# Order of TensorE's small products in an RWKV-7 recurrence: heads in turns, outputs by shape, a narrow projection on all rows

## The chip, the cores and the metric

The kernel runs on one core of one Trainium2 chip. The metric is the device time of one execution in microseconds (us); the median of three runs is given.

## The reference

A two-layer decoder trunk over 1024 tokens of 1024 channels in float32. Layer 0 is forgetting attention with a pooling mixer, layer 1 is RWKV-7 time mixing; each is followed by a SwiGLU feed-forward part with 2816 hidden channels. The change touches layer 1 alone:

```python
w = -jax.nn.softplus(-(w0 + jnp.tanh(xw @ w1) @ w2)) - 0.5      # narrow projections: 1024 -> 64 -> 1024
a = jax.nn.sigmoid(a0 + (xa @ a1) @ a2)
...
def _rwkv7_step(state, inp):                                     # 16 heads of 64 channels, 1024 tokens
    r_t, w_t, k_t, v_t, a_t, b_t = inp
    sa = jnp.einsum('bhvk,bhk->bhv', state, a_t)
    state = state * w_t[:, :, None, :] + sa[..., None] * b_t[:, :, None, :] + v_t[..., None] * k_t[:, :, None, :]
    return state, jnp.einsum('bhvk,bhk->bhv', state, r_t)
```

## The kernel before

Values lie with the channels on the partitions and the tokens along the free axis, in two halves of 512 tokens. A large product is made of 128x128 blocks of weights that are split into a high and a low part (`load_part`, lines 150 and 151: a copy on ScalarE, a difference on VectorE) and three passes on TensorE (`mm3`, lines 162 to 164). One such pass over 512 tokens is called a **fill pass** below.

The recurrence is cut into chunks of 64 tokens. `job(grp, half)` does four pairs of heads over half of the tokens; there are four jobs. A pair has one head on partitions 0 to 63 and the other on 64 to 127. A job has three stages:

- **Preparation**, pair by pair. After some elementwise work come the scores (line 1056: for each head two tiles of four products, 64 rows by 128 columns of the array, each 128 wide), their evictions (lines 1060 on ScalarE, 1061 and 1063 on VectorE), the transposes of `bk` (line 1069: eight for each head, 64 rows by 128 columns, 64 wide) and the values less their mean (line 1079: 64 rows by 64 columns, the two heads in turns). The tiles of the scores come from a pool of three PSUM banks (tag `s`), those of the transposes and values from a pool of two (tag `o`).
- **Inverses** of triangles, mostly 30 steps on VectorE (lines 1104 and 1106).
- **Chunks**, eight in a row: `z` (line 1159) and its copy, `u` (line 1165) and its copies, `sp` (line 1171), the next state on VectorE (lines 1173 to 1178), and the output `yp` (lines 1182 and 1184). Lines 1159, 1171 and 1182 use 128 rows by 64 columns, lines 1165 and 1184 use 64 by 64. In `yp` the two shapes take turns: two products of line 1182, two of line 1184, four times over.

Each job is woven with feed-forward work or projections: wherever the job says `yield n`, n more fill passes are emitted (`weave`; the numbers are in `fr`). The framework's scheduler then places each engine's instructions by readiness and priority, so the order on TensorE is its order, not quite the written one. A float32 product of the recurrence is one instruction in the program and two in the trace; a transpose is one in both.

The dense part of the layer (`dense`) has two narrow projections (`lora`), each with a hidden width of 64, for each half of the tokens. Their hidden values are stacked: high parts on rows 0 to 63 and low parts on rows 64 to 127 of a tile `t`, and the weights lie twice above each other. Each of eight blocks is a product of 128 rows (line 854) and one of 64 rows (line 855).

Of the kernel before, what the change touches and what calls it, by code (L numbers as in the profile page):

```python
# [19 lines left out]
S = 1024  # L20
# [7 lines left out]
# columns of the per-channel vector array  # L28
# [12 lines left out]
# columns of the constant array  # L41
# [34 lines left out]
def xtile(k, pool):  # L76
    """A tile of a half of the tokens with one column before them."""
    return pool.tile([P, HN + 1], F32, tag="x", name=nm(k, "x"), bufs=8)
# [46 lines left out]
def pmm(k):  # L125
    """A bank for a dense product of the stream that is being emitted."""
    pool, tag, bufs = k.mm
    return pool.tile([P, HN], F32, tag=tag, name=nm(k, tag), bufs=bufs)
# [6 lines left out]
def load_w(k, ap, tag="w", w=512, bufs=None, pool=None):  # L135
    """Loads a block of weights, 512 columns at a time, and splits each into two parts of which the sum is the block."""
    p, n = ap.shape
    return [load_part(k, ap[:, c:c + min(512, n)], p, min(512, n), tag, w, bufs, pool) for c in range(0, n, 512)]
# [16 lines left out]
def mm3(k, out, pairs, first=True, last=True):  # L155
    """out = sum of (wh + wl)^T (xh + xl) without wl^T xl, which is below float32's last bit.

    A generator: it yields the passes that it has put on the tensor engine."""
    nc = k.nc
    n = len(pairs)  # L160
    for i, ((wh, wl), (xh, xl)) in enumerate(pairs):
        nc.tensor.matmul(out, wh, xh, start=(first and i == 0), stop=False)  # L162
        nc.tensor.matmul(out, wh, xl, start=False, stop=False)  # L163
        nc.tensor.matmul(out, wl, xh, start=False, stop=(last and i == n - 1))  # L164
        yield 3


def narrow(k, out, n, w, xs):
    """float32 products with n columns of weights: 128 / n groups of columns of the array sum over a part of the inputs each."""
    g = P // n  # L170
    for c in range(0, len(xs), g):
        for q in range(g):
            j = c + q
# [5 lines left out]
def fold(k, out, src, n, tmp):  # L179
    """The sum of what narrow left in the groups of rows of src, on the first n rows."""  # L180
# [8 lines left out]
def run(gen):  # L189
    """Emits all of a generator; returns what it returns."""  # L190
# [12 lines left out]
def stream(k, i):  # L203
    """What follows runs where the streams of a lower number leave room."""
# [5 lines left out]
def ahead(fill, n):  # L210
    """Emits the first n passes of fill."""
    while n > 0:
        n -= next(fill)


def weave(main, *fills):
    """Emits main with as many passes of the fills as it asks for; a fill comes with its share, or alone."""
# [9 lines left out]
def using(k, gen, **own):  # L227
    """gen with settings of its own."""
# [20 lines left out]
def pair(k, pool, tag, bufs, n=HN):  # L249
    """The tiles of the two parts of a value."""  # L250
# [12 lines left out]
def use_ln_exp(k, after=None):  # L263
    """Has Exp and Ln read one table; after: the instruction whose table it replaces."""
# [6 lines left out]
def head_mean(k, sq, hl, more):  # L271
    """Mean over the channels of each head of a pair and a product more; hl: tiles for the parts of sq."""
# [8 lines left out]
class Norm:  # L281
    """RMS norm over the channels of [channel, token] tiles of one half of the tokens."""
# [30 lines left out]
def fox(k, ins, H, hpool, xpools, y, then, r_att):  # L313
    """The mixer of the first layer; y gets the tiles of its output, H those of its input.

    The projections take the tokens before their RMS norm; what it divides them by comes in behind the products.
    then runs beside the last pair of heads."""
# [22 lines left out]
    # of every half of the tokens: one over their root mean square, and what the heads' norms add for their own eps  # L340
# [34 lines left out]
    # operand tiles of the two heads of a pair  # L375
# [22 lines left out]
    def forget(half, wf):  # L398
        """Log sigmoid of the forget gates, running sums over the tokens."""
# [15 lines left out]
    def key_bias():  # L415
        """The running sums with the tokens on the partitions, negative."""
# [7 lines left out]
    def head(p, which, half, hl):  # L424
        """The queries or keys of a pair of heads."""
# [18 lines left out]
    def gate(p, half, hl):  # L444
        """The output's gate waits in the tile of the output."""
# [10 lines left out]
    def prep(p):  # L456
        """Projections of a pair of heads."""
# [37 lines left out]
    def maxima(p, a):  # L495
        h = 2 * p + a
        # cum of the keys along the free axis
# [26 lines left out]
    def attend(p, a):  # L524
        """Keys on the partitions, queries along the free axis; the values' products run behind the scores'."""
# [53 lines left out]
    def pool_group(g, half):  # L579
# [9 lines left out]
        # the mean over the tokens of a window comes after the product with the group's weights  # L589
# [92 lines left out]
def ffn(k, ins, L, halves, H, X, acc, tp, groups, after=None, silu=True, fb0=0):  # L682
# [25 lines left out]
    # the products with the third weights of a group run behind the first ones of the next  # L708
# [32 lines left out]
class Rwkv:  # L741
    """Time mixing of the second layer.

    The state runs over chunks of 64 tokens.  With L the running sum of the log decays inside a chunk,
    alpha_t = kk_t exp(L_{t-1}), beta_s = -kk_s a_s exp(-L_s), kt_s = k_s exp(-L_s), rt_t = r_t exp(L_t):
        U = (I - tril(alpha beta^T, -1))^-1 (alpha S + tril(alpha kt^T, -1) V)
        Y = rt S + tril(rt beta^T) U + tril(rt kt^T) V
        S <- exp(L_end) (S + beta^T U + kt^T V)
    The group norm's mean is taken off V, of whose rows every row of Y is a sum.
    """  # L750
# [11 lines left out]
    # ---- dense part  # L762
    def norm(self, half, rs, xt):
        """Puts the normalised tokens in the place of x, those of the token before beside them."""
# [35 lines left out]
    def sigmoid(self, t, src, j=None):  # L800
        """The sigmoid of src and column j of the vectors."""
# [8 lines left out]
    def dense(self, half, hd, mp, tp, which=((2, "k", 1), (3, "v", 4), (0, "r", 5))):  # L810
        """All projections of half of the tokens; the small ones run between the large ones."""
# [10 lines left out]
        def stacked(mx, w, n, func):  # L822
            """The hidden values of a narrow projection, high parts above low parts (above high parts)."""
# [23 lines left out]
        def lora(mx, w1, w2, func, c0, n):  # L847
            t = yield from stacked(mx, ins[w1], 64, func)
            for m in range(KT):
# [5 lines left out]
                nc.tensor.matmul(o, lo[0:64, c], t[0:64], start=False, stop=True)  # L855
# [3 lines left out]
        def stacked_w(w):  # L859
            """Weights for stacked hidden values: high parts twice above low parts."""  # L860
# [7 lines left out]
        def gate(mx, ts):  # L868
# [3 lines left out]
            for m in range(KT):  # L872
                # the first blocks start with what is there before the second part of the hidden values
# [28 lines left out]
        # a small projection runs among the blocks of a large one  # L902
# [22 lines left out]
    # ---- core  # L925
# [35 lines left out]
    def await_(self, n):  # L961
        """Asks for passes of the fills until n is there."""
# [3 lines left out]
    def head_sum(self, src):  # L966
        """The mean over the channels of each head of a pair."""
# [16 lines left out]
    def job(self, grp, half):  # L984
        """Four pairs of heads over half of the tokens.

        The rows of head h of a pair: its own half of the partitions (64 h to 64 h + 64) has what is summed over
        its channels or multiplies U, the other half what multiplies V, so that one product sums over both."""
# [14 lines left out]
        for i, p in enumerate(pr):  # L1003
# [6 lines left out]
            if i == 0:  # L1010
                ZL = [big(f"ZL{h}", 128) for h in range(2)]    # own: alpha | rt, other: alpha kt^T | rt kt^T
                XR = big("XR", 128)                            # own: inverse | rt beta^T
                SV = [big(f"SV{h}", 64) for h in range(2)]     # own: state, other: V
                BK = [big(f"BK{h}", 64) for h in range(2)]     # own: beta, other: kt
# [13 lines left out]
            # 1 / max(norm, 1e-12); what the bias adds is nothing beside 1e-24  # L1028
# [22 lines left out]
            # scores with the keys on the partitions: beta above kt, alpha beside rt  # L1051
            for h in range(2):
                for b in range(2):
                    sc = pst(k, "s", k.sbufs)
                    for c in range(4):
                        nc.tensor.matmul(sc[:, 128 * c:128 * c + 128], bk[HS[h], 4 * b + c], ZL[h][HS[h], i, 4 * b + c],  # L1056
                                         start=True, stop=True)
                    s4 = sc.rearrange("p (c t) -> p c t", t=128)
                    bs = slice(4 * b, 4 * b + 4)
# [6 lines left out]
            for h in range(2):  # L1066
                pt = pst(k, "o", 2)
                for c in range(8):
                    nc.tensor.transpose(pt[:, 64 * c:64 * c + 64], bk[HS[h], c], ident[HS[h], HS[h]])
# [15 lines left out]
        # inverses of the unit triangles: 32 x 32 blocks by substitution, one block a partition  # L1085
# [9 lines left out]
        # what lies above the diagonal, in squares, and the diagonal  # L1095
# [53 lines left out]
        for c in range(8):  # L1149
# [30 lines left out]
            for i in range(4):  # L1180
                for h in range(2):
                    nc.tensor.matmul(yp[HS[h], i], SV[h][:, i, c], ZL[h][:, i, c, 64:128], start=True, stop=False)  # L1182
                for h in range(2):
                    nc.tensor.matmul(yp[HS[h], i], uv[h][HS[h], i], XR[HS[h], i, c, 64:128], start=False, stop=True)  # L1184
# [5 lines left out]
        # the variances of all heads on a few rows, one over their roots in two parts there, then back to all rows  # L1190
# [39 lines left out]
def build(ctx, tc, ins, outs, dbg=None, stop=99):  # L1230
# [30 lines left out]
    # first layer's mixer  # L1261
# [23 lines left out]
    def oproj_early():  # L1285
        """What the output projection can do before the last pair of heads is there."""
# [91 lines left out]
    def tail(half, p, ng, silu):  # L1378
        """The last output projection and what follows it, for half of the tokens."""
# [76 lines left out]
def layout(inputs):  # L1456
    """The inputs in the order that the loads want."""
# [87 lines left out]
```

## Time and profile before

| | before |
|---|---|
| median of three runs | 2766.65 us (2763.74 to 2767.2) |
| span of the profiled execution, first to last instruction | 2762.1 us |
| PE (TensorE) busy | 2712.5 us (98%) |
| DVE (VectorE) busy | 1728.4 us (63%) |
| ACT (ScalarE) busy | 1300.0 us (47%) |
| mean granted TensorE clock | 0.998 |

The profiled execution has no time of its own beside its span; the span is 4.5 us below the median of the runs, which is what lies around it. Busy time of TensorE counts overlapping matmuls once. In the timeline the first column is the start of an instruction or of a run of like ones, the second its length to the end of the last; since matmuls overlap, what a matmul takes from the next is read from start to start.

### The profile page before, as it was taken

The page shows a single profiled execution, that of the slowest core. Times are in us where ns is not written, and L with a number is a line of the kernel's source. Part 1 is how long each engine was busy: PE and PEld are TensorE (multiplying, and loading weights), DVE is VectorE, ACT ScalarE, POOL GpSimd, SP SyncE. Part 2 cuts the span into 40 slices and gives each one's busy share as a digit, 9 for nine tenths or more (in the row PEclk, how much of TensorE's full clock was granted, in tenths as well). Part 3 has the DMA queues.
Part 4 walks back from the last instruction along what each step waited for, and adds up shares of the span by engine and source line. Part 5 has one row for each costly group of instructions (what it writes and reads, how often), then busy time and mean ns, then how long its engine had stood idle before and what let it go on. Part 6 is the DMA issues. An engine that isn't in the chain of part 4 may idle for free.

```text
span 2762.1 us, 40277 instructions
## 1 busy us (share of the span) xinstructions
PE 2712.5 (98%) x15368; PEld 2099.0 (76%) x15368; DVE 1728.4 (63%) x2940; ACT 1300.0 (47%) x2297; POOL 50.9 (2%) x139
## 2 busy tenths in 40 slices
PE   9999999999999999999999999999999999999999
PEld 6777778778887667777777676777777777788887
DVE  7777685653436655975984675469668846544343
ACT  7555664442225665434534466664445434333222
POOL 1000000000001000000000000000000000000000
PEclk9999999999999999999999999999999999999999
DMA  4111131233333445424433525454244235333332
GB/s 133 60 47 61 40 96 46 88 94 93 95 96 110 164 154 182 129 83 124 142 92 93 189 94 159 156 181 124 82 127 142 81 96 191 107 97 99 96 99 92
DMA packets 170241, 306.11 MB, mean 111 GB/s; under 512 B 18608, under 2 KB 25904, under 8 KB 170048
## 3 DMA queue, kind: packets, MB, share of 16 engines
q1 hardware_dynamic: 156224, 278.38, 32.8%
q10 hardware_dynamic: 13824, 25.17, 2.5%
q8 instruction: 120, 1.97, 0.3%
q14 instruction: 73, 0.60, 0.1%
HBM read 257.04 MB, written 46.43 MB: 110 GB/s over the span
## 4 chain that ended last, share of the span: by engine, by line
PE 84%; DVE 9%; ACT 2%; issue 2%; DMA 2%; SPq 0%; ACTq 0%; DVEq 0%
PE mm L162 17%; PE mm L163 16%; PE mm L164 16%; PE fm L162 7%; PE fm L164 6%; PE fm L163 6%; DVE wlo L151 2%; PE s L1056 2%; PE o L1184 1%; PE mm L174 1%; PE o L1182 1%; DVE nu L1106 1%; DVE pd L1104 1%; PE o L1171 1%; PE s L1159 1%
## 5 line engine op out<-in xcount | busy, mean ns | idle before, releaser
L150 ACT CAST whi<-wraw 128x512 fp32r<-128x512 f32 x738 | 453.4, 616 | 875.0 <-PE mm L163 494.5
L151 DVE TENSOR_TENSOR wlo<-wraw,whi 128x512 fp32r<-128x512 f32 x738 | 501.2, 683 | 465.7 <-ACT whi L150 454.2
L162 PE MATMUL mm<-hh,whi 128*128 128x512 f32 x864 | 344.8, 401 | 6.7 <-ACT hh L354 6.2
L164 PE MATMUL mm<-hh,wlo 128*128 128x512 f32 x864 | 340.3, 394 | 0.0
L163 PE MATMUL mm<-hl,whi 128*128 128x512 f32 x864 | 339.2, 394 | 0.0
L162 PE MATMUL mm<-uh,whi 128*128 128x512 f32 x728 | 289.2, 399 | 0.9 <-DVE x L1312 0.9
L164 PE MATMUL mm<-uh,wlo 128*128 128x512 f32 x728 | 287.1, 395 | 0.9 <-DVE wlo L151 0.9
L163 PE MATMUL mm<-ul,whi 128*128 128x512 f32 x728 | 287.3, 396 | 0.0
L162 PE MATMUL fm<-h1h,whi 128*128 128x512 f32 x528 | 217.6, 412 | 10.1 <-DVE sg L725 6.0
L164 PE MATMUL fm<-h1h,wlo 128*128 128x512 f32 x528 | 207.7, 393 | 0.0
L163 PE MATMUL fm<-h1l,whi 128*128 128x512 f32 x528 | 207.6, 393 | 0.1
L162 PEld LDWEIGHTS mm<-hh,whi 128*128 128x128 f32 x864 | 162.8, 189 | 43.2 <-ACT hh L354 6.9
L164 PEld LDWEIGHTS mm<-hh,wlo 128*128 128x128 f32 x864 | 162.7, 188 | 36.0 <-DVE wlo L151 0.4
L163 PEld LDWEIGHTS mm<-hl,whi 128*128 128x128 f32 x864 | 163.1, 189 | 33.1 <-DVE hl L355 1.1
L162 PE MATMUL fm<-hh,whi 128*128 128x512 f32 x416 | 173.6, 417 | 1.9 <-ACT hh L258 1.9
L162 PEld LDWEIGHTS mm<-uh,whi 128*128 128x128 f32 x728 | 136.3, 187 | 42.2 <-issue 7.0
L163 PE MATMUL fm<-hl,whi 128*128 128x512 f32 x416 | 166.3, 400 | 0.2 <-DVE hl L259 0.2
L164 PE MATMUL fm<-hh,wlo 128*128 128x512 f32 x416 | 166.0, 399 | 0.0
L163 PEld LDWEIGHTS mm<-ul,whi 128*128 128x128 f32 x728 | 136.5, 187 | 34.9 <-issue 1.1
L164 PEld LDWEIGHTS mm<-uh,wlo 128*128 128x128 f32 x728 | 136.5, 187 | 34.3 <-DVE wlo L151 1.3
L704 DVE TENSOR_TENSOR x<-mm,x 128x512 f32<-128x512 f32 x96 | 66.2, 692 | 122.9 <-PE mm L164 122.6
L162 PEld LDWEIGHTS fm<-h1h,whi 128*128 128x128 f32 x528 | 98.9, 187 | 42.6 <-issue 8.8
(338 smaller groups left out, 4731.0 us busy)
## 6 DMA issues: line engine op xcount, KB each, us to landing
wraw<-in_wg_dram SPq DMA_DIRECT2D x176, 256.0 KB, 2.8
wraw<-in_wu_dram SPq DMA_DIRECT2D x176, 256.0 KB, 2.7
wraw<-in_wd_dram SPq DMA_DIRECT2D x176, 256.0 KB, 2.7
wraw<-in_w_in_dram SPq DMA_DIRECT2D x52, 256.0 KB, 3.0
x<-in_xT_dram SPq DMA_DIRECT2D x32, 256.0 KB, 4.8
x<-x SPq DMA_DIRECT2D x32, 256.0 KB, 3.8
wraw<-in_w_k_dram SPq DMA_DIRECT2D x32, 256.0 KB, 2.9
wraw<-in_w_v_dram SPq DMA_DIRECT2D x32, 256.0 KB, 2.8
```

The costliest lines, as they stand in the source:

```text
L150: k.nc.scalar.copy(hi[0:p, 0:n], raw[0:p, 0:n])
L151: k.nc.vector.tensor_tensor(lo[0:p, 0:n], raw[0:p, 0:n], rd(hi[0:p, 0:n]), ALU.subtract)
L162: nc.tensor.matmul(out, wh, xh, start=(first and i == 0), stop=False)
L163: nc.tensor.matmul(out, wh, xl, start=False, stop=False)
L164: nc.tensor.matmul(out, wl, xh, start=False, stop=(last and i == n - 1))
L174: k.nc.tensor.matmul(out[n * q:n * q + n], w[:, n * j:n * j + n], xs[j], start=c == 0, stop=c + g == len(xs), tile_position=(0, n * q))
L704: nc.vector.tensor_tensor(X[half][m], o, X[half][m], ALU.add)
L1056: nc.tensor.matmul(sc[:, 128 * c:128 * c + 128], bk[HS[h], 4 * b + c], ZL[h][HS[h], i, 4 * b + c], start=True, stop=True)
L1104: nc.vector.tensor_tensor(pv, nu[:, j + 1:32, j:j + 1].broadcast_to([P, n, j]), nu[:, j:j + 1, 0:j].broadcast_to([P, n, j]), ALU.mult)
L1106: nc.vector.tensor_tensor(nu[:, j + 1:32, 0:j], nu[:, j + 1:32, 0:j], pv, ALU.add)
L1159: nc.tensor.matmul(z[HS[h], i], ZL[h][:, i, c, 0:64], SV[h][:, i, c], start=True, stop=True)
L1171: nc.tensor.matmul(sp[HS[h], i], BK[h][:, i, c], uv[h][:, i], start=True, stop=True)
```

## The change

The two heads of a pair take turns in the scores and in the transposes, so that the banks of a pair's scores are asked for two at a time, and both banks of its transposes at once. The products of `yp` come in two groups, eight of line 1182 and then eight of line 1184; the first of each head's column group starts the sums and the last ends them. The low weights of a narrow projection are multiplied by all 128 rows of `t`, which adds their product with the low parts. Comments are left out throughout the new file; of that nothing is shown.

```diff
@@ lora
                 nc.tensor.matmul(o, hi[:, c], t, start=True, stop=False)
-                nc.tensor.matmul(o, lo[0:64, c], t[0:64], start=False, stop=True)
+                nc.tensor.matmul(o, lo[:, c], t, start=False, stop=True)
@@ job
-            for h in range(2):
-                for b in range(2):
-                    sc = pst(k, "s", k.sbufs)
-                    for c in range(4):
-                        nc.tensor.matmul(sc[:, 128 * c:128 * c + 128], bk[HS[h], 4 * b + c], ZL[h][HS[h], i, 4 * b + c],
+            for b in range(2):
+                scs = [pst(k, "s", k.sbufs) for _ in range(2)]
+                for c in range(4):
+                    for h in range(2):
+                        nc.tensor.matmul(scs[h][:, 128 * c:128 * c + 128], bk[HS[h], 4 * b + c], ZL[h][HS[h], i, 4 * b + c],
                                          start=True, stop=True)
-                    s4 = sc.rearrange("p (c t) -> p c t", t=128)
-                    bs = slice(4 * b, 4 * b + 4)
+                bs = slice(4 * b, 4 * b + 4)
+                for h in range(2):
+                    s4 = scs[h].rearrange("p (c t) -> p c t", t=128)
...
-            for h in range(2):
-                pt = pst(k, "o", 2)
-                for c in range(8):
-                    nc.tensor.transpose(pt[:, 64 * c:64 * c + 64], bk[HS[h], c], ident[HS[h], HS[h]])
+            pts = [pst(k, "o", 2) for _ in range(2)]
+            for c in range(8):
+                for h in range(2):
+                    nc.tensor.transpose(pts[h][:, 64 * c:64 * c + 64], bk[HS[h], c], ident[HS[h], HS[h]])
+            for h, pt in enumerate(pts):
...
             yp = i3(pst(k, "o", 2))
-            for i in range(4):
-                for h in range(2):
-                    nc.tensor.matmul(yp[HS[h], i], SV[h][:, i, c], ZL[h][:, i, c, 64:128], start=True, stop=False)
-                for h in range(2):
-                    nc.tensor.matmul(yp[HS[h], i], uv[h][HS[h], i], XR[HS[h], i, c, 64:128], start=False, stop=True)
+            for i, h in ihs:
+                nc.tensor.matmul(yp[HS[h], i], SV[h][:, i, c], ZL[h][:, i, c, 64:128], start=i == 0, stop=False, skip_group_check=True)
+            for i, h in ihs:
+                nc.tensor.matmul(yp[HS[h], i], uv[h][HS[h], i], XR[HS[h], i, c, 64:128], start=False, stop=i == 3, skip_group_check=True)
```

The scheduled order on TensorE for a pair's scores (`s<-ZL,bk`), transposes (`o<-cc,bk`) and values (`o<-cc,ld`), third pair of the last job, before; rows of fill passes are left out where "..." stands:

```order
L1056 MATMUL s_19606<-ZL_4170_19109,bk_19594 128x128 x4
L1056 MATMUL s_19631<-ZL_4170_19109,bk_19594 128x128 x4
L1056 MATMUL s_19645<-ZL_4171_19110,bk_19594 128x128 x4
...
L1056 MATMUL s_19667<-ZL_4171_19110,bk_19594 128x128 x4
...
L1069 MATMUL o_19684<-cc,bk_19594 128x64 x8
...
L1069 MATMUL o_19708<-cc,bk_19594 128x64 x8
...
L1079 MATMUL o_19725<-cc,ld_19602 64x64 x16
```

The same pair with the change:

```order
L1057 MATMUL s_19606<-ZL_4170_19109,bk_19594 128x128
L1057 MATMUL s_19607<-ZL_4171_19110,bk_19594 128x128
...
L1057 MATMUL s_19606<-ZL_4170_19109,bk_19594 128x128
L1057 MATMUL s_19607<-ZL_4171_19110,bk_19594 128x128
L1057 MATMUL s_19645<-ZL_4170_19109,bk_19594 128x128 x4
...
L1057 MATMUL s_19646<-ZL_4171_19110,bk_19594 128x128 x4
L1071 MATMUL o_19684<-cc,bk_19594 128x64
L1071 MATMUL o_19685<-cc,bk_19594 128x64
...
L1082 MATMUL o_19725<-cc,ld_19602 64x64 x16
```

The first eight products take turns. The next two tiles do not: with three banks only one of them can be had, so one head's four products follow in a row, and the other head's four come after the first bank has been emptied. The sixteen transposes stand together. Over all 16 pairs, the stretches in which scores, transposes or values interrupt the fill passes go from 75 to 61, and the number of fill passes in each stage stays the same.

The output of the first chunk of the first job on TensorE, before, behind the products of `sp` (line 1171):

```order
L1182 MATMUL o_10960<-ZL_2218_9416,SV_2221_9419 64x64
L1182 MATMUL o_10960<-ZL_2219_9417,SV_2222_9420 64x64
L1184 MATMUL o_10960<-XR_9418,uv_10897 64x64
L1184 MATMUL o_10960<-XR_9418,uv_10898 64x64
L1182 MATMUL o_10960<-ZL_2218_9416,SV_2221_9419 64x64
L1182 MATMUL o_10960<-ZL_2219_9417,SV_2222_9420 64x64
```

The end of it with the change:

```order
L1185 MATMUL o_10960<-ZL_2219_9417,SV_2222_9420 64x64
L1185 MATMUL o_10960<-ZL_2218_9416,SV_2221_9419 64x64
L1185 MATMUL o_10960<-ZL_2219_9417,SV_2222_9420 64x64
L1187 MATMUL o_10960<-XR_9418,uv_10897 64x64
L1187 MATMUL o_10960<-XR_9418,uv_10898 64x64
L1187 MATMUL o_10960<-XR_9418,uv_10897 64x64
L1187 MATMUL o_10960<-XR_9418,uv_10898 64x64
```

All products of one shape stand together; what comes ahead of them and behind them in a chunk has not moved.

## Rows read from the trace of the kernel before

**Rows 1.** The page, part 1: busy time, share, instructions of each engine.
```profile
PE 2712.5 (98%) x15368; PEld 2099.0 (76%) x15368; DVE 1728.4 (63%) x2940; ACT 1300.0 (47%) x2297; POOL 50.9 (2%) x139
```

**Rows 2.** Windows: stretch, length; PE, PEld, DVE, ACT, POOL busy; clock; DMA share; GB/s.
```profile
910.00:950.00 40.00, 40.00 (x160) 29.09 (x159) 21.95 (x34) 27.71 (x49) 0.00 (x0) 1.00 0.57 188
1074.00:1142.00 68.00, 64.79 (x446) 49.20 (x444) 63.88 (x101) 38.70 (x72) 4.53 (x9) 1.00 0.49 154
...
1213.00:1290.00 77.00, 77.00 (x823) 56.72 (x822) 35.96 (x70) 29.59 (x64) 0.79 (x2) 1.00 0.32 94
1307.00:1372.00 65.00, 63.10 (x420) 48.52 (x419) 61.25 (x96) 38.31 (x69) 1.99 (x7) 1.00 0.51 158
...
1815.00:1890.00 75.00, 71.70 (x448) 55.22 (x447) 62.94 (x100) 49.11 (x88) 3.18 (x9) 0.98 0.56 180
...
2066.00:2140.00 74.00, 74.00 (x485) 56.04 (x485) 66.38 (x103) 41.23 (x77) 2.89 (x7) 1.00 0.48 145
```

**Rows 3.** Timeline, PE, first chunk: start, length, instruction, shape, count.
```profile
1213.67 0.69 PE L1159 MATMUL s<-SV,ZL 128*64 128x64 f32 x16
1214.29 0.50 PE L162 MATMUL fm<-h1h,whi 128*128 128x512 f32 x1
...
1215.88 0.68 PE L1165 MATMUL s<-zs,XR 64*64 64x64 f32 x16
1216.49 0.50 PE L162 MATMUL fm<-h1h,whi 128*128 128x512 f32 x1
...
1218.75 0.69 PE L1171 MATMUL o<-uv,BK 128*64 128x64 f32 x16
1219.27 0.29 PE L1182 MATMUL o<-ZL,SV 128*64 128x64 f32 x4
1219.48 0.33 PE L1184 MATMUL o<-XR,uv 64*64 64x64 f32 x4
...
1221.33 0.50 PE L971 MATMUL t<-ph,bones 128*128 128x512 f32 x1
...
1223.38 0.69 PE L1159 MATMUL s<-SV,ZL 128*64 128x64 f32 x16
```

**Rows 4.** Timeline, DVE, the next chunk's state.
```profile
1220.42 0.86 DVE L1177 TENSOR_TENSOR SV<-st,Pc 64x256 f32<-64x256 f32 x2
```

**Rows 5.** Timeline, PE, third pair of the last job.
```profile
2109.32 2.60 PE L1056 MATMUL s<-ZL,bk 64*128 64x128 f32 x24
2111.86 0.49 PE L164 MATMUL fm<-gh,wlo 128*128 128x512 f32 x1
2112.28 1.16 PE L1056 MATMUL s<-ZL,bk 64*128 64x128 f32 x8
2113.37 0.50 PE L162 MATMUL fm<-gh,whi 128*128 128x512 f32 x1
...
2114.27 0.71 PE L1069 MATMUL o<-cc,bk 64*128 64x64 f32 x8
2114.91 0.50 PE L162 MATMUL fm<-gh,whi 128*128 128x512 f32 x1
```

**Rows 6.** Timeline, PE, two score tiles in a row, third job.
```profile
1846.94 2.05 PE L1056 MATMUL s<-ZL,bk 64*128 64x128 f32 x16
1848.92 0.51 PE L163 MATMUL fm<-hl,whi 128*128 128x512 f32 x1
```

**Rows 7.** Timeline, PE, the longest wait of a score tile for its bank.
```profile
1089.22 1.13 PE L1056 MATMUL s<-ZL,bk 64*128 64x128 f32 x8 [1.31 <-DVE ZL L1063]
```

**Rows 8.** Timeline, PE, one block of a narrow projection between fill passes.
```profile
912.55 0.39 PE L854 MATMUL mm<-st,wlhi 128*128 128x512 f32 x1
912.89 0.50 PE L855 MATMUL mm<-st,wllo 64*128 64x512 f32 x1
913.32 0.50 PE L162 MATMUL mm<-uh,whi 128*128 128x512 f32 x1
913.65 0.39 PE L163 MATMUL mm<-ul,whi 128*128 128x512 f32 x1
913.88 0.40 PE L164 MATMUL mm<-uh,wlo 128*128 128x512 f32 x1
```

**Rows 9.** Groups by line and shape, PE: count, busy us, mean ns, idle before.
```profile
L855 PE MATMUL mm<-st,wllo 64*128 64x512 f32 x32 | 15.9, 498 | 0.0
```

## The prediction

> **What bounds the kernel now.** I read the page's busy times first: TensorE is busy for 98% of the span [rows 1], so what it no longer does is time gained, unless it then waits. Whether it would wait differs by stage, so I read the windows next [rows 2]. In a chunk stage (1213 to 1290, one of four) TensorE is busy all 77.00 us and VectorE 35.96: TensorE alone sets the pace. The same holds among the blocks of a narrow projection (910 to 950). In the preparation of pairs it is otherwise: VectorE has 63.88 of 68 us, 61.25 of 65, 62.94 of 75 and 66.38 of 74. There both engines are nearly full, and a gain on TensorE is worth at most what VectorE has left. Last I read the timelines, start to start, because busy times hide how far matmuls overlap. They show one thing that carries most of the sum: TensorE pays whenever the shape of its tiles changes. A fill pass starts 0.23 us after the one before it [rows 8]; around other shapes the steps are longer.
>
> **The outputs, by shape.** Before, 16 products of `yp` run from 1219.27 to 1221.33, which is 2.06 us, with eight changes of shape counting the one that leaves [rows 3]. For the new order each group has a neighbour of its own shape and number. Line 1185 continues the shape of `sp`: 16 instructions of line 1171 took 0.52 from start to start, 0.05 of it the entry, so 0.47. Line 1187 has the shape of `u`: 0.61 from its start to the fill pass behind it, both edges in it [rows 3]. The step from the first group to the second costs about 0.1 more: the first four of line 1182 took 0.21 instead of 0.12. Together 1.18, so 0.88 less in a chunk, and four jobs of eight chunks make 32: **28.2 us**. Does a wait take its place? The next `z` needs the state, which VectorE has ready at 1221.28 [rows 4], while `z` starts at 1223.38 [rows 3]. Moved up by 0.88 it still starts 1.2 us later than that. The weights' work on ScalarE and VectorE has room in this stage, since both are busy for less than half of it [rows 2]. I count all of it.
>
> At this place a rule of the skill speaks against the change. In line 1187 the two heads sit on different rows of the array and write to one bank. The Trainium skill, TensorEngine Tiling (Array Packing), Restrictions and Gotchas, says that different row tiles cannot access the same PSUM bank at the same time. By that rule the two heads of line 1187 would go one after the other, which is the fourth rival below. The trace differs: line 1165 has the same shape, the same rows and one bank, and needs 0.61 for 16 instructions [rows 3], 0.04 each with both edges in it.
>
> **The narrow projections.** From line 854 to the second fill pass behind line 855 it is 1.10 us for three steps (912.55 to 913.65) that would take 0.70 in one shape [rows 8]. So a product of 64 rows costs 0.40 more than one of 128. There are 32 [rows 9]: 12.8 us. A few of them lie in the second dense part, where norms are waited for too; I take **11.5**. Nothing else changes there, since the low weights are loaded for all 128 rows anyway.
>
> **Scores and transposes.** A score instruction takes a slot of 0.112 us while its rows of the array are in use: 16 take 1.98 [rows 6], 8 take 1.09 [rows 5]. An interruption of the fill passes costs 0.19 more at its edges (2111.86 to 2112.28 is 0.42 instead of 0.23). That different heads overlap is to be seen already: the 24 in a row take 2.54 [rows 5], which is 0.56 more than 16, five slots for eight instructions. Where the second head comes in, it runs beside the end of the first. In the new order the first 16 instructions of a pair should take 8 slots, the next eight 8 more (one head alone), the last eight 8.
>
> A typical pair before: 2.54 + 0.19, 1.09 + 0.19, and two times 0.64 + 0.19 for the transposes, 5.67 us [rows 5]. With the change: 16 slots as in rows 6, 1.98 + 0.19; one head's tile, 1.09 + 0.19; and 16 transposes in the time of eight, 0.64 + 0.19; in all 4.28. That is 1.39 less in a pair and 22.2 in 16. Some pairs are cut into more pieces before and gain more, some have transposes beside scores already and gain less; the order has 75 interruptions before and 61 now, about one less in a pair, so the typical pair stands for all.
>
> How much of this is kept? A job saves 5.6 on TensorE. VectorE has left 4.1 us in the first preparation, 3.8 in the second, 12.1 in the third and 7.6 in the fourth [rows 2], and its work does not change. I take half of the first two, 2 each, and 5 each of the others: **14 us**. The bounds are 0 and 22.2.
>
> The pool of three banks adds no wait in the typical pair. The fourth tile waits for the eviction of the first, and the first is complete after 8 slots, as before. It started 2.96 us after the first (2109.32 to 2112.28) [rows 5], and now would be asked for after 1.98 and a few fill passes. In the first pair of the first job it waited 1.31 for VectorE [rows 7], and there the wait grows by what the scores save. Behind it on TensorE stand the values and all fill passes. That is in what I left out of the 22.2. VectorE, ScalarE and the load queue get the same instructions as before in a somewhat other order; the DMA engines are busy for half of these stretches, so I count that at nothing. If a late load lets a fill pass wait, it costs what the load is late.
>
> **The sum.** 28.2 + 11.5 + 14 = 53.7, from a span of 2762.1 to 2708.4. The median of the runs lies 4.5 above the span, so 2713.
>
> **The rivals.**
> - *VectorE holds the preparation.* All of the 14 is lost to waits for VectorE. For it: its 94% in the first two preparations. Against: TensorE is busy for all 74.00 us of the fourth [rows 2]. 28.2 + 11.5 gives 2727.
> - *Everything is kept.* 28.2 + 12.8 + 22.2 = 63.2, 2703. For it: the third and fourth have room. Against: the first two.
> - *Heads in turns don't overlap,* so that the change does not do what it says in scores and transposes. Then a pair saves one interruption, 0.34, 5 in all and half of it kept: 28.2 + 11.5 + 2.5, 2724. Against it: the five slots for eight.
> - *Two row tiles in one bank exclude each other* in line 1187. Eight more steps of about 0.06 (a transpose's 0.64 / 8 is no less) in each of 32 chunks are 16 us: 2729. Against it: line 1165. This is the rule of the Trainium skill, TensorEngine Tiling (Array Packing), named above.
> - *Slower: the fourth score tile.* Both tiles of a group are now emptied together, VectorE has no room, and TensorE stands at the fourth bank in every pair. It decides from 53.7 / 16 = 3.4 us a pair on; at 4 us it gives 2777. The longest such wait now is 1.31 [rows 7].
>
> **How the numbers follow.** Forecast 0.63, VectorE 0.15, everything 0.13, no overlap 0.04, banks 0.03, slower 0.02. The range reaches from the second rival, less a microsecond for the runs' scatter, to the first, plus one: 2702 to 2728; it leaves out a part of the banks' case, the slower one and what I have not thought of. A measurement of this kernel tells 0.2%, 5.5 us, from no change. All cases but the last are faster by more: 0.97. Same 0.01, slower 0.02.
>
> **What would show it.** Outputs: 1.2 us from the first instruction of line 1185 to the pass behind line 1187, with one wide step inside, and chunks 0.9 us shorter. Narrow projections: steps of 0.23 throughout. Scores: the first 16 in pairs some nanoseconds apart, 1.8 us for 24. TensorE's idle time before lines 1057 and 1026 and the fill passes of the preparation should grow, by some 8 us in all, and VectorE's share there should rise towards 100%. I am wrong if chunk stages do not get shorter by 7 us each, or if the idle time grows by more than 20.

## The result, and the profile after

The changed kernel takes 2725.0 us (median of four runs, 2721.09 to 2726.04) against 2765.19 for the kernel before in the same measurement: a ratio of 0.9853, interval 0.9841 to 0.9865. Faster, as forecast, by 40 us instead of the 53.7 of the forecast; 2725.0 lies inside the range of 2702 to 2728 and near its upper end. The span went from 2762.1 to 2723.9 us, by 38.2.

The head of the page after answers to [rows 1]: TensorE is busy for 47 us less, and still for 98% of the span.

```profile
span 2723.9 us, 40262 instructions
## 1 busy us (share of the span) xinstructions
PE 2665.5 (98%) x15368; PEld 2080.5 (76%) x15368; DVE 1725.1 (63%) x2940; ACT 1297.9 (48%) x2297; POOL 50.0 (2%) x139
```

The timeline of TensorE in the first chunk of the first job, after (start, length, instruction, shape, count), answers to [rows 3]:

```profile
1218.31 0.69 PE L1174 MATMUL o<-uv,BK 128*64 128x64 f32 x16
1218.82 0.64 PE L1185 MATMUL o<-ZL,SV 128*64 128x64 f32 x16
1219.39 0.68 PE L1187 MATMUL o<-XR,uv 64*64 64x64 f32 x16
1220.00 0.50 PE L971 MATMUL t<-ph,bones 128*128 128x512 f32 x1
...
1222.05 0.69 PE L1162 MATMUL s<-SV,ZL 128*64 128x64 f32 x16
```

From 1218.82 to 1220.00 it is 1.18 us for all the outputs, the forecast's figure, and nothing waits behind them. The first chunk stage takes 68.77 us instead of 75.81 by these windows, before and after (TensorE is busy for all of both), and the four together are 28.1 us shorter.

```profile
1213.67:1289.48 75.81, 75.81 (x817) 56.17 (x816) 35.93 (x69) 29.07 (x63) 0.79 (x2) 1.00 0.32 95
1213.23:1282.00 68.77, 68.77 (x818) 52.38 (x817) 35.73 (x69) 28.95 (x63) 1.00 (x2) 1.00 0.33 105
```

A block of a narrow projection, after, by the timeline of TensorE, answers to [rows 8]:

```profile
916.90 0.39 PE L854 MATMUL mm<-st,wlhi 128*128 128x512 f32 x1
917.12 0.40 PE L855 MATMUL mm<-st,wllo 128*128 128x512 f32 x1
917.36 0.39 PE L162 MATMUL mm<-uh,whi 128*128 128x512 f32 x1
917.59 0.40 PE L163 MATMUL mm<-ul,whi 128*128 128x512 f32 x1
```

The steps are 0.22 to 0.24, 0.69 for three instead of 1.10. Over all 32 blocks these three steps add up to 34.2 us before and 22.7 after; the two dense parts together are 10 to 11 us shorter.

The third pair of the last job, after, answers to [rows 5]:

```profile
2078.14 2.05 PE L1057 MATMUL s<-ZL,bk 64*128 64x128 f32 x24
2080.12 0.50 PE L164 MATMUL fm<-gh,wlo 128*128 128x512 f32 x1
```

Twenty-four score instructions take 1.98 us instead of 2.54, sixteen slots as priced. Sixteen transposes in turns, after, take 0.64 from start to start, as eight did before [rows 5]:

```profile
1118.51 0.71 PE L1071 MATMUL o<-cc,bk 64*128 64x64 f32 x16
1119.15 0.50 PE L162 MATMUL fm<-h1h,whi 128*128 128x512 f32 x1
```

So each part does on TensorE what was foreseen. What it brought there is another matter. For the stretch of each job from the first product of line 1026 to the first `z` (preparation and inverses), the windows before and after (length; busy time of PE, of PEld, which is TensorE's loading of weights, of DVE, ACT and POOL; clock; DMA share; GB/s) are these. Before:

```profile
1077.11:1213.67 136.56, 130.21 (x989) 101.42 (x989) 125.77 (x213) 70.84 (x127) 5.04 (x13) 1.00 0.39 117
1307.92:1450.75 142.83, 136.21 (x1018) 106.55 (x1016) 130.49 (x220) 69.47 (x125) 4.53 (x14) 1.00 0.40 121
1825.97:1963.36 137.39, 131.90 (x980) 102.50 (x980) 124.70 (x211) 72.33 (x129) 4.49 (x15) 0.98 0.38 116
2058.11:2201.26 143.15, 139.79 (x1017) 107.44 (x1015) 129.45 (x218) 73.83 (x134) 4.27 (x15) 1.00 0.40 123
sum 559.93, PE 538.11 PEld 417.90 DVE 510.40 ACT 286.47 POOL 18.32; mean PE 134.53 PEld 104.48 DVE 127.60 ACT 71.62 POOL 4.58
```

After:

```profile
1071.40:1213.23 141.83, 132.58 (x990) 103.69 (x990) 125.26 (x213) 70.85 (x127) 4.50 (x13) 0.94 0.36 113
1300.46:1441.35 140.89, 133.13 (x1018) 103.74 (x1016) 130.04 (x220) 69.90 (x125) 3.90 (x14) 0.99 0.40 124
1805.16:1939.25 134.09, 126.02 (x979) 97.21 (x979) 124.12 (x211) 71.53 (x129) 3.92 (x15) 0.99 0.38 117
2026.99:2169.61 142.62, 137.11 (x1017) 105.80 (x1015) 128.57 (x218) 73.99 (x134) 4.08 (x15) 0.96 0.40 124
sum 559.43, PE 528.84 PEld 410.44 DVE 507.99 ACT 286.27 POOL 16.40; mean PE 132.21 PEld 102.61 DVE 127.00 ACT 71.57 POOL 4.10
```

The four stretches take 559.93 us before and 559.43 after. Three numbers explain that. Waits are the length less TensorE's busy time: 21.8 before, 30.6 after. What the clock took is (1 - clock) times the length, added up by row: 3 before, 17 after. What remains is TensorE's work at full clock: 535 before and 512 after. So by this sum TensorE has 23 us less to do in scores and transposes, where 22.2 was priced, and gets back 9 as waits and 14 at the half clock. The clock knows two levels here, 2.4 and 1.2 GHz; in the profile before it was at the lower one for 6.8 us of these stretches, after for 34.1. The sum counts all of that time as half lost, which is somewhat too much: the outputs-alone run below, whose first stretch has the same instructions as before, puts the loss at about 0.4 us for each us at the lower level, so the 14 is nearer 11 and the 23 nearer 20. After, each of the six times at the lower level begins in a wait of TensorE of 1.3 to 4.0 us or shortly behind one; ten other waits of 0.8 us or more in these stretches were not followed by one.

Where the waits are is told by the waits of TensorE, here those of the recurrence after (1000 to 2300: total, times, longest):

```profile
PE fm L162 <- DVE sg L725: 11.1, 7, 4.0
PE s L1057 <- DVE ZL L1065: 6.0, 6, 1.7
...
PE s L1057 <- DVE bk L1041: 2.8, 4, 0.9
```

Before, the first two of these stood at 7.3 and 2.4:

```profile
PE fm L162 <- DVE sg L725: 7.3, 5, 2.8
...
PE s L1056 <- DVE ZL L1063: 2.4, 3, 1.3
```

The longest one, in the timeline of TensorE after:

```profile
1183.58 0.39 PE L164 MATMUL fm<-h1h,wlo 128*128 128x512 f32 x1
1188.00 0.80 PE L162 MATMUL fm<-h1h,whi 128*128 128x512 f32 x1 [4.04 <-DVE sg L725]
1188.60 0.63 PE L163 MATMUL fm<-h1l,whi 128*128 128x512 f32 x1
1189.02 0.63 PE L164 MATMUL fm<-h1h,wlo 128*128 128x512 f32 x1
```

and VectorE beside it:

```profile
1180.24 4.05 DVE L1115 STREAM_TRANSPOSE XR<-nu 32x1024 f32<-32x1024 f32 x2
1184.33 1.29 DVE L151 TENSOR_TENSOR wlo<-wraw,whi 128x512 fp32r<-128x512 f32 x2
1185.54 1.89 DVE L1115 STREAM_TRANSPOSE XR<-nu 32x1024 f32<-32x1024 f32 x1
1187.30 0.65 DVE L725 TENSOR_TENSOR sg<-fm,sg 128x512 f32<-128x512 f32 x1
```

A fill pass waits for a 0.65 us operation that stands in VectorE's queue behind transposes of about 2 us. Behind the wait the fill passes step by 0.42 instead of 0.23: the clock was granted at half.

### The profile page after: what moved, and what is told of

Read it like the earlier page. It is cut to its first block, busy times and chain, and to the rows that moved or that the text cites. A ratio compares the mean times of both kernels' runs of the same rounds, so it can differ in the third digit from the quotient of the medians.

```text
span 2723.9 us, 40262 instructions
## 1 busy us (share of the span) xinstructions
PE 2665.5 (98%) x15368; PEld 2080.5 (76%) x15368; DVE 1725.1 (63%) x2940; ACT 1297.9 (48%) x2297; POOL 50.0 (2%) x139
## 4 chain that ended last, share of the span: by engine, by line
PE 82%; DVE 11%; ACT 3%; DMA 2%; issue 2%; SPq 0%; ACTq 0%; DVEq 0%
PE mm L162 17%; PE mm L163 16%; PE mm L164 16%; PE fm L162 7%; PE fm L164 6%; PE fm L163 6%; DVE wlo L151 2%; PE mm L174 1%; DVE nu L1109 1%; DVE pd L1107 1%; PE s L1057 1%; PE o L1174 1%; PE s L1162 1%; PE s L1168 1%; PE o L1187 1%
```

## The experiments

The first theory, A, was the forecast's own, sharpened: VectorE's time is the bound in these stretches. Theory B was that the saving there is real and is lost only where it meets the other two parts. Four kernels went first, three of them one part of the change alone.

**Outputs alone.**

```diff
-            for i in range(4):
-                for h in range(2):  ... yp <- SV, ZL
-                for h in range(2):  ... yp <- uv, XR
+            for i, h in ihs:  ... yp <- SV, ZL
+            for i, h in ihs:  ... yp <- uv, XR
```

> The kernel before with the outputs yp summed shape by shape and nothing else changed. Both theories: the four chunk stages of 76 us each lose 7 us, 28 us in all, about 2737. If part of the chunk stages' gain was paid back in the next preparation (a later load, VectorE behind), less than 25.

Measured: 2737.77, ratio 0.9891 (0.9873 to 0.9909), 30 us of 2768.55. The chunk stages each lost 7.0. This run shows something else. Its first preparation is the kernel before's, instruction for instruction, and yet its first stretch took 142.45 us instead of 136.56, with less waiting (5.37 instead of 6.35) and a clock of 0.94, which is 17.1 us at the lower level, where the profile before has none in this stretch:

```profile
1076.69:1219.14 142.45, 137.08 (x989) 106.96 (x989) 125.80 (x213) 70.88 (x127) 4.86 (x13) 0.94 0.36 112
```

The timeline of TensorE there has the wait of [rows 7] again, 1.30 instead of 1.31, and then the values (line 1079) at the lower clock, 1.92 us instead of 1.15. Before:

```profile
1090.71 1.15 PE L1079 MATMUL o<-cc,ld 64*64 64x64 f32 x32
```

In this run:

```profile
1088.81 1.13 PE L1056 MATMUL s<-ZL,bk 64*128 64x128 f32 x8 [1.30 <-DVE ZL L1063]
1089.77 0.59 PE L1069 MATMUL o<-cc,bk 64*128 64x64 f32 x7
1090.29 1.92 PE L1079 MATMUL o<-cc,ld 64*64 64x64 f32 x32
```

The clock fell behind this wait in one execution and not in the other. Over the stretch TensorE was busy for 6.87 us more with the same instructions, 0.4 us for each of the 17.1 at the lower level.

**Scores and transposes alone.**

```diff
-            for h in range(2):
-                for b in range(2):  ... four products of one head, then their eviction
+            for b in range(2):  ... four products of each head in turns, then both evictions
...
-            for h in range(2):  ... eight transposes of one head
+            for c in range(8):  ... a transpose of each head
```

> The kernel before with heads in turns in scores and transposes and nothing else changed. Theory A (in preparation and inverses the 22 us that TensorE saves turn into waits for VectorE, and into stretches at the half clock that those waits bring on): between -4 and +4 us against before. Theory B (the saving of scores and transposes is real, and only its meeting with the other two parts loses it): 14 to 22 us faster, about 2745 to 2752.

Measured: 2762.88, ratio 0.9981 (0.9972 to 0.999), 5 us. Theory B is out; theory A's figure, no more than 4, is missed by a microsecond or two. By the windows, TensorE's work in the four stretches fell by 22 as in the changed kernel, waits rose from 21.8 to 30.4, and the clock took 15. Nor is the lower clock one profile's chance: the eleven runs of this kernel have a mean clock of 0.9935, the fifteen of the kernel before beside them 0.9954.

**Narrow projections alone.**

```diff
-                nc.tensor.matmul(o, lo[0:64, c], t[0:64], start=False, stop=True)
+                nc.tensor.matmul(o, lo[:, c], t, start=False, stop=True)
```

> The kernel before with the low weights of the narrow projections multiplied by all rows and nothing else changed. Both theories: 32 x 0.39 us less by the steps of the trace, of which the changed kernel shows 10 to 11 between its marks; 10 to 12 us faster, about 2755. If the dense parts waited for something else, under 6.

Measured: 2756.76, ratio 0.9954 (0.9938 to 0.997), 12 to 13 us: all of it kept. The three parts alone add up to 1.74% of the time, the change makes 1.47%; the intervals allow the two to be the same.

**Less work for VectorE.**

```diff
-                    nc.vector.tensor_tensor(XR[HS[h], i, bs, 64:128], s4[HS[0], :, 64:128],
-                                            self.msk[HS[0], 1:2].broadcast_to([64, 4, 64]), ALU.mult)
+                    nc.scalar.activation(XR[HS[h], i, bs, 64:128], s4[HS[0], :, 64:128], AF.Copy, scale=0.0)
```

> The changed kernel with one VectorE operation of each score tile (64 of 0.415 us, the mask of rt beta^T) replaced by a ScalarE copy times zero, so that the part of the output that comes from rt beta^T is left out. TensorE's work is the same. Theory A: VectorE was the bound in the preparation, so of its 26.6 us less 10 to 22 show in the time, with fewer waits of TensorE and fewer stretches at the half clock: 2703 to 2715. Theory B: no more than 4 us against the changed kernel's 2725.

Measured: 2724.55, ratio 0.984 (0.9824 to 0.9857), half a microsecond from the changed kernel. In the four stretches:

```profile
sum 557.94, PE 523.00 PEld 406.28 DVE 483.97 ACT 302.69 POOL 16.67; mean PE 130.75 PEld 101.57 DVE 120.99 ACT 75.67 POOL 4.17
```

VectorE was busy for 484 us instead of 508, TensorE's work was the same, and the length did not move: waits rose to 34.9 and the clock took 11. Theory A falls with this: less work for VectorE as a whole did not shorten the stretches. The edit gives ScalarE a second operation on each score tile (302.69 us busy instead of 286.27), and whether that hid a gain was not tested; no wait of TensorE for that operation stands in the trace.

The next theory, C: TensorE waits for chains of results, and the 22 us were their cover, so that more fill passes would restore it. Three kernels changed and one before had more of them.

```diff
-    rw.fr = [6, 6, 5, 16, 7, 9, 16], [7, 7, 4, 16, 7, 8, 20]
+    rw.fr = [6, 7, 6, 16, 7, 9, 16], [7, 8, 5, 16, 7, 8, 20]    # more in both; also in the kernel before
+    rw.fr = [6, 8, 5, 16, 7, 9, 16], [7, 9, 4, 16, 7, 8, 20]    # preparation alone
+    rw.fr = [6, 6, 6, 16, 7, 9, 16], [7, 7, 5, 16, 7, 8, 20]    # inverses alone
```

> The changed kernel with one fill pass more at each place in the scores and transposes (6 to 7 and 7 to 8) and in the inverses (5 to 6 and 4 to 5), some 60 passes more in each job and as many fewer after it. Theory C (TensorE waits for a chain of results and for banks, not for VectorE's time; the 22 us that it saved were the cover of those waits): waits and half clock in preparation and inverses, 47 us in the changed kernel, fall by 13 to 25; 2700 to 2712. Theory A (VectorE's time is the bound): each fill pass brings VectorE work along, 2720 to 2730.

> The changed kernel with two fill passes more at each place in the scores and transposes alone (6 to 8 and 7 to 9), 56 in each job. Theory C: only the waits of the preparation (14.7 us, and 6.8 lost at the half clock) can go; 8 to 15 us, 2710 to 2717. Theory A: 2720 to 2730.

> The changed kernel with one fill pass more at each step of the inverses alone (5 to 6 and 4 to 5), 33 in each job. VectorE is busy for 96% there in every run so far, so theory A says 2722 to 2730 for this one even if the preparation is not bound by VectorE; theory C, that the waits of 14.6 us there are for fill operands that stand behind long operations, says 2712 to 2720.

> The kernel before with the same more fill passes as the changed kernel had in both stages. Theory C: fewer waits to cover (25 us with the half clock), 4 to 12 us faster, 2753 to 2762, so that the two kernels with more fill are 46 to 60 us apart instead of 40. Theory A: no gain and again some 40 us apart.

Measured: more in both 2756.27, ratio 0.9959 (0.9944 to 0.9974); preparation alone 2740.22, 0.9905 (0.9888 to 0.9922); inverses alone 2733.71, 0.9882 (0.9865 to 0.99); the kernel before with more in both 2793.17, 1.0097 (1.0079 to 1.0115). Every one is slower than the kernel that it came from, by 31, 15, 9 and 28 us. Theory C is out, and theory A's figures are missed as well. (The expectation's 96% for VectorE in the inverses holds for the first job; by windows over the inverses of the changed kernel the other three have 93 to 94%.) The four stretches with more in both:

```profile
sum 632.53, PE 594.10 PEld 462.93 DVE 535.12 ACT 309.23 POOL 17.11; mean PE 148.52 PEld 115.73 DVE 133.78 ACT 77.31 POOL 4.28
```

Waits are 38.4 instead of 30.6, though there was more to do between them. More work beside them did not cover them; many of them are waits of the fill passes themselves, 17.6 us for `sg` alone. About half of the 31 us lies outside the stretches, which have fewer passes in their place: TensorE's waits there rose from 27.8 to 41.3 us, and the time at the lower clock from 10 to 22. So the run's time is no measure of these stretches alone; the waits in them are.

So the opposite, theory D: fewer fill passes.

```diff
+    rw.fr = [6, 5, 5, 16, 7, 9, 16], [7, 6, 4, 16, 7, 8, 20]    # preparation
+    rw.fr = [6, 6, 4, 16, 7, 9, 16], [7, 7, 3, 16, 7, 8, 20]    # inverses
```

> The changed kernel with one fill pass less at each place in the scores and transposes (6 to 5 and 7 to 6), 28 fewer in each job and as many more after it. Theory D (TensorE waits there for operands of the fill passes themselves and for banks, which stand in VectorE's queue behind the job's own work; a denser stretch has more of it, as the runs with more fill showed): fewer waits, 2712 to 2722. Theory C (the passes are cover, and less cover means more waiting): 2728 to 2740.

> The changed kernel with one fill pass less at each step of the inverses (5 to 4 and 4 to 3), 33 fewer in each job. Theory D: VectorE is busy for 96% there, partly with work of the fill passes; with less of that the inverses end sooner and TensorE waits less for fill operands: 2710 to 2722. Theory C: TensorE, which has fewer passes beside VectorE's 30 steps, waits for their end: 2728 to 2745.

Measured: less in the preparation 2736.35, ratio 0.9886 (0.9866 to 0.9906), slower than the changed kernel by 11; waits rose to 41, so here the passes did cover something, as theory C had it. Less in the inverses 2726.48, 0.985 (0.9831 to 0.987), no difference, and between the two forecasts. In that one the four stretches look so:

```profile
1070.52:1199.69 129.17, 121.68 (x953) 95.10 (x953) 120.51 (x206) 69.22 (x124) 4.51 (x13) 0.96 0.39 118
1287.40:1420.79 133.39, 126.18 (x980) 98.47 (x978) 125.72 (x214) 69.63 (x125) 3.92 (x14) 0.97 0.41 125
1797.35:1927.81 130.46, 123.15 (x944) 94.64 (x944) 119.46 (x205) 68.65 (x124) 3.92 (x15) 0.93 0.36 113
2015.55:2150.86 135.31, 129.70 (x981) 100.21 (x980) 123.44 (x211) 70.48 (x129) 4.19 (x14) 0.95 0.39 124
```

Their waits are 27.6, three less than the changed kernel's, and the clock took 24 to 25 instead of 17. What the waits gave, the clock took. So neither more fill passes nor fewer help, and theory D is out for both stages.

**Scores head by head again**, the rest as changed:

```diff
-            for b in range(2):  ... four products of each head in turns, then both evictions
+            for h in range(2):
+                for b in range(2):  ... four products of one head, then their eviction
```

> The changed kernel with the scores head by head as before, and transposes, outputs and narrow projections as changed. If the turns of the scores bring waits for banks and the half clock for as much as they save (some 10 of the 22 us): 2721 to 2729, no difference from the changed kernel. If their saving is real: 2732 to 2737.

Measured: 2726.01, ratio 0.9852 (0.9831 to 0.9873), the same as the changed kernel's 0.9853. This is the run that settles the scores: their turns are worth nothing in time that these runs can tell, which is some 6 us; their saving on TensorE is about 14. The four stretches show where it went:

```profile
1070.94:1208.16 137.22, 129.53 (x989) 101.55 (x990) 125.90 (x213) 70.84 (x127) 5.14 (x13) 0.99 0.39 117
1295.39:1438.59 143.20, 136.29 (x1017) 106.52 (x1015) 130.05 (x220) 68.75 (x125) 4.70 (x14) 0.99 0.40 122
1802.18:1936.27 134.09, 127.20 (x980) 99.11 (x980) 124.38 (x211) 71.72 (x129) 4.06 (x15) 1.00 0.39 120
2023.95:2169.39 145.44, 139.73 (x1017) 107.64 (x1015) 129.46 (x218) 74.05 (x134) 4.50 (x15) 0.98 0.39 120
sum 559.95, PE 532.75 PEld 414.82 DVE 509.80 ACT 285.36 POOL 18.40; mean PE 133.19 PEld 103.71 DVE 127.45 ACT 71.34 POOL 4.60
```

Against the changed kernel TensorE has some 15 us more work here (527, by 532.75 less the 6 that the clock took), 3 us fewer waits and 11 us less at the half clock, in 559.95 us instead of 559.43. The clock differs in the runs too: 0.995 to 0.996 in these four, 0.992 in three of the changed kernel's four. The transposes were not tried without the scores.

**Scores by head and less fill in the inverses together**, both edits as above:

> The changed kernel with the scores head by head again and one fill pass less at each step of the inverses. Theory G (the time of these stages is TensorE's work, plus its waits, plus what stretches at the half clock lose; scores by head keep the clock up, 6.8 us lost instead of 16.4, and less fill in the inverses takes some 3 us of waits away): 2710 to 2720, faster than either edit alone. If the waits or the clock give back whatever is saved, as in the three runs around 2726: 2721 to 2730.

Measured: 2725.42, ratio 0.9848 (0.9826 to 0.987). The median says no gain; the sum that theory G expected (TensorE's work, plus waits, plus what the clock takes) did not come out, because the clock in its profile took 24 us and not 7. Its five runs are the clearest on what goes with the time: 2718.21 and 2720.36 at a mean clock of 0.996 and 0.997, 2725.42 at 0.994, 2729.91 and 2730.41 at 0.990 and 0.991. No version was clearly faster than the changed kernel.

## Why the prediction was right, and where it was not

- **The outputs by shape**: right in every figure, 1.18 us a chunk and 28.2 priced against 28.1 measured between marks, 30 with an interval of 5 on either side as a part alone. The fourth rival is refuted: line 1187 has both heads in one bank, and 16 instructions of it take 0.61, as forecast. The Trainium skill (TensorEngine Tiling (Array Packing), Restrictions and Gotchas) says that different row tiles cannot access one bank at the same time; for these tiles the trace does not agree.
- **The narrow projections**: 11.5 taken, 11.5 by the steps of the 32 blocks, 10 to 11 between marks, and 13 with an interval of 4 on either side as a part alone.
- **Scores and transposes**: the price was right, 22.2 against 20 to 23 of TensorE's work. The step that failed is the one behind it, "I take half of the first two, 2 each, and 5 each of the others: 14 us". Kept was 0.5 in the two profiles, where the four stretches changed by +5.3, -1.9, -3.3 and -0.5 us, and 5 as a part alone. The time measured is near the first rival's, 2727, with half of its cause. TensorE's waits rose by 9, most of them for VectorE, as the forecast said they should, by some 8. But the rival and I read VectorE's share as its lack of time, and taking 24 us from it changed nothing. And the sum has no term for the clock: the table ahead of it gave 0.998 for the profile before, and the 11 to 14 us that the clock took were put at nothing without a reason.
- **The total**: the forecast itself, 2713, was missed by 12 us. That the time lies in the range is owed to the first rival, whose time the range took in, and not to the forecast's third term.
- **The signs**: VectorE's share in the preparation was to rise towards 100%; by windows over the four preparations it went from 93 to 94%. The idle time before line 1026 was to grow; it fell from 4.6 to 2.5 us. The "1.8 us for 24" scores contradicts the working, whose own 1.98 is what was measured.
- **The fourth score tile**: the wait for its bank did grow, from 2.4 to 6.0 us in all, longest 1.7. It is far from the 3.4 a pair that the slower rival needed.

What the runs show is this account: in these stretches the length is TensorE's work, its waits, and what the clock takes; in the two profiles the 20 to 23 us went from the first to the other two. No run held the clock, but runs at the same mean clock can be set side by side. At 0.994 four runs of scores and transposes alone have a median of 2762.9 us, nine of the kernel before 2771.1: 8 us are kept there, more than the 5 of all runs and far from 22. At 0.995 the changed kernel's one run took 2721.09, five of the kernel before 2769.0: 48 us instead of 40. So the clock takes a part and the waits another. At the same clock the 22 less the 9 of the waits would leave 13, and 8 were kept; what took the other 5 stays open. What stays open as well is why the waits answer to so little. They are for single results in VectorE's queue, as at 1187.30; another order of that queue, which the scheduler makes, was not tried.

## What to carry to other kernels

Put small matmuls of one tile shape together, and fill an idle half of the rows if that keeps the shape: each change of shape cost 0.1 to 0.2 us here, and where TensorE alone sets the pace all of it comes back. In a stretch where TensorE waits at all, price a saving on it at nothing until the waits are named one by one, and read the granted clock beside them, in more than one run. A busy share of another engine near 95% is not proof that its time is the bound; take some of its work away and see.

## What was not expected of the hardware

The clock goes with the scatter of the runs. Of 46 timed runs of the kernel before, ten had a mean clock of 0.998 and a median of 2762.7 us, nine had 0.994 and 2771.1: 2.1 us for each 0.001. In the eleven runs of scores and transposes alone it is 0.8, so the price is not one for all kernels. The mean over the runs was 0.996 before and 0.993 for the changed kernel, so at 2.1 its typical loss to the clock is estimated at 6.6 us more, less than in the two profiles, since the one profile before that was read was among those with a high clock. Behind one and the same wait of 1.3 us the clock fell in one execution and not in another. The Trainium skill (TensorE: Matmul & The Clock Gate, Part 1) says that the window in which the chip judges activity runs freely and does not start with the program. That would let the same program meet it differently each time; no run here shows the window itself.

Two heads on different rows of the array overlap fully in float32, transposes included: 24 score instructions of which 16 are in turns take sixteen slots, 1.98 us, and sixteen transposes in turns took the time of eight, 0.64.
